# An expert-weight ring over all staging buffers, the spill branch between the expert groups, and a one-hot scatter in two passes

## The chip, the cores and the metric

The kernel runs on one core of one Trainium2 chip. The metric is the time of one execution on the device in microseconds, taken as the median of several runs. All data is 32-bit; TensorE (PE) multiplies it either as plain float32 or, where both operands are typed fp32r, in one shortened pass. Where full precision is wanted from fp32r, the kernel splits a value into a high part and a low remainder and multiplies both.

## The reference, cut to what matters

Two decoder layers over 256 tokens of width 1024. The change lies in the second layer's channel mixer, a top-2-of-8 mixture of experts, and in what follows it:

```python
def moe(x, router, wg, wu, wd):
    xt = x.reshape(-1, dm)
    logits = (xt @ router).astype(jnp.float32)
    top_v, top_i = lax.top_k(logits, TOP_K)
    w = jax.nn.softmax(top_v, axis=-1)
    gate = jnp.sum(jax.nn.one_hot(top_i, N_EXPERTS) * w[..., None], axis=1)
    for e in range(N_EXPERTS):
        out = out + gate[:, e:e + 1] * swiglu(xt, wg[e], wu[e], wd[e])
...
    h = h + f
    h = h + (p[i] @ ple_proj[i]) * jax.nn.sigmoid(rmsnorm(h, g_ple[i]) @ ple_gate[i])
return rmsnorm(h, g_final)
```

Each expert has three matrices of 1024 x 3584 in float32. All eight experts are read once: 336 pieces of 1 MiB.

## The kernel before

**Expert layer.** The experts are handled in two groups g of four. For each group a one-hot matrix `sm` (built on VectorE, DVE, by `select`) picks the tokens of its experts into 3 blocks of 128 slots: two blocks hold 64 fixed slots per expert, the third two units of 32 slots that go to whichever experts have more tokens. `gather` multiplies the token matrix (as the pair `xhi`, `xlo`) by the one-hot into `xg`. Then seven column blocks m of 512 hidden columns follow: 8 stretches of `wg`, 8 of `wu`, and 8 of `wd` (two halves n of 4). A stretch is 1 MiB: 128 rows, 512 columns for each of the four experts. `quad` multiplies it: 8 matmuls with 512 columns, four of them side by side in the array, and 4 with 256 columns for the third block, whose weights `unit_weights` copies out of the stretch (one copy on ScalarE, ACT, one on DVE, with the expert's number read from a register). `turn` transposes the hidden block, `down` adds to the group's result `Y`. The down product of block m-1 stands behind the up product of block m. After a group's last `down`, `scatter` multiplies `Y` by the transposed one-hot `sT` (already scaled by the routing gate in `back`) in plain float32, and `settle` adds the result to the residual `h`.

**Weight buffers.** SyncE (SP) issues all weight loads, in order. `stretch` takes one of the 8 `raw` buffers of a pool (`load`, L167), used in turn; a load waits until the buffer's last reader is through. The first layers' weights use the same pool, and also split each raw buffer into `hi` and `lo` (3 buffers each; `split`, L193 and L194). In the expert layer `hi` and `lo` serve only for the small unit copies (L1028, L1029). Once, after the eighth stretch, three spare tiles (`pp`, `Y`, `xn`; L1017) are filled as well.

**Spill.** Tokens that do not fit into the blocks would be handled by `spill`, inside `tc.If` on a flag that is read from the routing. It stands twice, one behind the other, between the last block's `turn` and its `down`. In the runs here the flag is zero and both are skipped. Instructions behind a `tc.If` are not moved ahead of it; otherwise the framework's scheduler orders the instructions of each engine.

**After the experts.** `aside` is the embedding projection (`ple_proj`: one 1 MiB weight load, split, 24 matmuls), placed in the last column block. Then `ple` follows in a written order: it loads four 1 MiB pieces of the gate matrix (`gate_of`), splits the first two, settles the second half of the last scatter, transposes and multiplies, adds to `h`, and the final norm goes out. `Norm.gains` (L242) loads a norm's gain vector, and L780 the input `p`.

Of the kernel before, what the change touches and what calls it, by code (L numbers as in the profile page):

```python
# [92 lines left out]
def trunk(ctx: ExitStack, tc: tile.TileContext, a, cst, at, out, stop=None):  # L93
# [66 lines left out]
    def load(src, shape, behind=None, parts=1):  # L160

        n = shape[0] * shape[1]
        raw = rawp.tile([128, 2048], F32, name="raw")
        v = raw[:, :n].rearrange("p (a b) -> p a b", b=shape[1])
        m = shape[0] // parts
        for j in range(0, shape[0], m):
            order(nc.sync.dma_start(v[:, j:j + m], src[:, j:j + m]), behind)  # L167
        return raw, v
# [60 lines left out]
    class Norm:  # L229
# [10 lines left out]
        def gains(self, c=slice(0, D)):  # L240
            n = c.stop - c.start
            nc.sync.dma_start(self.g[:, c], bass.AP(tensor=self.src.tensor, offset=self.src.offset + c.start,  # L242
                                                    ap=[[0, 128], [1, n]]))
            return self
# [532 lines left out]
    def ple_proj(i, pool, keep, name="pT", bufs=1, out="pp"):  # L777

        pin = nrm.tile([128, NT, PLE], F32, name="junk")
        nc.sync.dma_start(pin, a["p"][i, 0].rearrange("(t p) d -> p t d", p=128))  # L780
# [52 lines left out]
    def moe(i, pool, N, after, aside):  # L833
# [106 lines left out]
        def select(g):  # L940
# [15 lines left out]
            return [g, sm, None, None, xp.tile([128, KC, 3, 128], F32, name="xg")]  # L956

        def factors(G):

            g, sm = G[:2]  # L960
            G[2] = gs = xp.tile([128, 4, 2], F32, name="gs", bufs=2)
# [9 lines left out]
            own = xp.tile([128, 4, GRP], F32, name="own", bufs=2)  # L971
            mask = xp.tile([128, 2, GRP], F32, name="mask", bufs=2)
            nc.vector.tensor_copy(gs[:, 0:3, 0], pv[:, :, GRP])
            nc.vector.tensor_copy(gs[:, 3, 0:1], gs[:, 2, 0:1])
# [5 lines left out]
            for half in range(2):  # L980
                nc.vector.scalar_tensor_tensor(own[:, 2 + half], pv[:, 2, 0:GRP], K["half"][:, half:half + 1], mask[:, 0],
                                               op0=ALU.mult, op1=ALU.mult)
# [3 lines left out]
        def back(G):  # L986

            sm, gs = G[1:3]
            G[3] = sT = xp.tile([128, 4, S], F32, name="sT")
            for b in range(3):  # L990
# [3 lines left out]
                for j in ((b,) if b < 2 else (2, 3)):  # L994
                    nc.scalar.activation(sT[:, j], p[:, 0:S], AF.Copy, scale=gs[:, j, 1:2])
# [12 lines left out]
        count, held = [0], {}  # L1008
# [15 lines left out]
        def unit_weights(g, w):  # L1024

            hi = hip.tile([128, 2048], F32R, name="hi").bitcast(F32)[:, 0:512]
            lo = lop.tile([128, 2048], F32R, name="lo").bitcast(F32)[:, 0:512]
            nc.scalar.copy(hi, w[:, bass.ds(units[g][0], 1), :].rearrange("p e n -> p (e n)"))  # L1028
            nc.vector.tensor_copy(lo, w[:, bass.ds(units[g][1], 1), :].rearrange("p e n -> p (e n)"))  # L1029
            return hi, lo  # L1030
# [11 lines left out]
        def column(src, G, m, new, ahead=None):  # L1042
# [3 lines left out]
            for k in range(KC):  # L1046
                w = stretch(src[G[0], m, k])
                if ahead is not None and k + 1 < KC:
# [4 lines left out]
        def turn(H):  # L1053
            hT = xp.tile([128, 4, 3, 128], F32, name="hT", bufs=2)
# [13 lines left out]
        def down(G, m, hT, Y, n, new):  # L1068

            P = [new() for b in range(3)]  # L1070
            for c in range(4):
                w = stretch(wd[G[0], m, n, c])
                quad(G[0], P, hT[:, c], w, c == 0, c == 3)
            for b in range(3):
                y = Y[:, b, n * WIDE[b]:(n + 1) * WIDE[b]]
# [5 lines left out]
        def scatter(G, Y, t, n, p):  # L1081

            for b in range(2):
                nc.tensor.matmul(p, G[3][:, b, t * 128:(t + 1) * 128], Y[:, b, n * 512:(n + 1) * 512], start=(b == 0),  # L1084
                                 stop=False, skip_group_check=True)
            for half in range(2):
                nc.tensor.matmul(p[:, half * 256:half * 256 + 256], G[3][:, 2 + half, t * 128:(t + 1) * 128],  # L1087
                                 Y[:, 2, n * 256:(n + 1) * 256], start=False, stop=True, skip_group_check=True)
# [6 lines left out]
        def spill(base):  # L1095
# [8 lines left out]
            sg = xp.tile([128, 512], F32, name="H0")  # L1104
# [5 lines left out]
            def fetch(src):  # L1110
# [4 lines left out]
            for e in range(NE):  # L1115
# [22 lines left out]
                for m in range(FCH):  # L1138
                    po = []
                    for src in (wg, wu):  # L1140
                        po.append(bank())
                        for k in range(KC):
                            fetch(src[g, m, k, :, j, :])
# [8 lines left out]
                    for c in range(4):  # L1152
                        for n in range(2):
                            fetch(wd[g, m, n, c, :, j, :])
# [19 lines left out]
        Y = xp.tile([128, 3, D], F32, name="Y")  # L1174
        pp = xp.tile([128, 2048], F32, name="pp")
        spare = [pp, Y.rearrange("p b n -> p (b n)")[:, 0:2048], nrm.tile([128, 2048], F32, name="xn")]
        ahead_of = {j: (wg, wu)[j // KC][0, 0, j % KC] for j in range(RAWS, 2 * KC)}
# [6 lines left out]
        for g in range(NE // GRP):  # L1184
            for m in range(FCH):
                first, final = g + m == 0, g + 1 == NE // GRP and m + 1 == FCH
                if m == 0 and g:
                    G = select(g)
# [10 lines left out]
                if last is not None:  # L1199
                    for t in range(NT):  # L1200
                        for n in range(2):
                            settle(t, n, scatter(last, Y, t, n, bank()))
# [154 lines left out]
```

## Time and profile before

| | us |
|---|---|
| median of 3 runs | 1515.51 |
| lowest, highest | 1510.32, 1520.99 |
| profiled execution | 1517.39 |
| its span | 1515.6 |

Over the span PE is busy 1449.3 us (96%), DVE 642.1 (42%), ACT 569.8 (38%), and the DMA engines move 462.39 MB, on average 305 GB/s. PE's busy time overlaps from one matmul to the next and is no measure of how full the array is; the expert layer, from about 615 to 1476 us, is better read by what its stretches wait for and by the DMA rate in each stage. Times in rows are microseconds from the span's start.

### The profile page before, as it was taken

Reading aid. Unit: us, or ns where it says so; the run is one execution under the profiler, and the core shown is the slowest. Engines: PE = TensorE matmul, PEld = TensorE weight load, DVE = VectorE, ACT = ScalarE, POOL = GpSimd, SP = SyncE. Lnnn points to the kernel's source line nnn. Section 1 sums busy time; section 2 is a strip of 40 time slices with the busy share of each in tenths; the row PEclk is TensorE's granted clock in tenths of the full one; section 3 lists DMA queues with packets and bytes.
Section 4 is the critical chain, followed back from the end, with each engine's and each line's share of the span. In section 5 each row is a group of like instructions: output and inputs, shape, how many; then the busy total and the mean of one; then the engine's idle time right before and its main releaser. Section 6 shows DMA issues by size and latency. Waiting matters only on the chain. (4 is left out here: it accounts for less than half of the span.)

```text
span 1515.6 us, 30676 instructions
## 1 busy us (share of the span) xinstructions
PE 1449.3 (96%) x12570; PEld 832.9 (55%) x12570; DVE 642.1 (42%) x1459; ACT 569.8 (38%) x992; POOL 2.3 (0%) x8
## 2 busy tenths in 40 slices
PE   7999999999999999899999999999999999999987
PEld 6977899999889868433322232243333323323336
DVE  6765865555596767323222222222221322322337
ACT  5452544434464543333332332333233223223324
POOL 0000000000000000000000000000000000000000
PEclk9998999999999999899999999999999999999999
DMA  9923445555557513789999999999999999999971
GB/s 332 365 86 97 160 167 194 190 179 188 169 179 252 199 57 146 250 346 420 420 420 420 419 421 420 420 419 416 405 383 420 420 419 420 419 421 420 412 273 42
DMA packets 100621, 462.39 MB, mean 305 GB/s; under 512 B 9384, under 2 KB 20336, under 8 KB 57200
## 3 DMA queue, kind: packets, MB, share of 16 engines
q1 hardware_dynamic: 100224, 460.16, 77.5%
q8 instruction: 102, 1.67, 0.4%
q14 instruction: 55, 0.45, 0.1%
q10 hardware_dynamic: 240, 0.10, 0.0%
HBM read 459.19 MB, written 1.05 MB: 304 GB/s over the span
## 5 line engine op out<-in xcount | busy, mean ns | idle before, releaser
L1029 DVE COPY lo<-raw 128x512 f32 x333 | 140.7, 426 | 544.5 <-DMA raw<-in_moe_up 152.3
L1028 ACT COPY hi<-raw 128x512 f32 x333 | 204.0, 621 | 429.5 <-DMA raw<-in_moe_down 129.2
L194 DVE TENSOR_TENSOR lo<-raw,hi 128x1024 fp32r<-128x1024 f32 (+1 forms) x176 | 206.6, 1200 | 111.7 <-ACT hi L193 111.1
L193 ACT CAST hi<-raw 128x1024 fp32r<-128x1024 f32 (+1 forms) x176 | 175.0, 1031 | 170.0 <-issue 71.8
L1039 PE MATMUL w<-raw,xg 128*32 128x512 f32 x1744 | 211.5, 596 | 12.3 <-DMA raw<-in_moe_up 5.0
L1039 PE MATMUL acc<-raw,xg 128*32 128x512 f32 x1792 | 214.7, 596 | 2.5 <-DMA raw<-in_moe_gate 0.6
L207 PE MATMUL w<-xhi,hi 128*128 128x256 f32 x704 | 201.2, 286 | 0.3 <-ACT xhi L283 0.3
L209 PE MATMUL w<-xhi,lo 128*128 128x256 f32 x704 | 199.9, 284 | 0.0
L208 PE MATMUL w<-xlo,hi 128*128 128x256 f32 x704 | 199.7, 284 | 0.2 <-DVE xlo L284 0.2
L207 PEld LDWEIGHTS w<-xhi,hi 128*128 128x128 f32 x704 | 135.0, 192 | 2.4 <-issue 1.6
L208 PEld LDWEIGHTS w<-xlo,hi 128*128 128x128 f32 x704 | 135.0, 192 | 1.3 <-issue 0.8
L209 PEld LDWEIGHTS w<-xhi,lo 128*128 128x128 f32 x704 | 135.0, 192 | 0.8 <-issue 0.8
L1039 PE MATMUL acc<-raw,hT 128*32 128x512 f32 x960 | 116.6, 603 | 11.6 <-PEq L1225 6.6
L1039 PEld LDWEIGHTS w<-raw,xg 128*32 128x32 f32 x1744 | 51.8, 109 | 117.1 <-issue 66.2
L1039 PEld LDWEIGHTS acc<-raw,xg 128*32 128x32 f32 x1792 | 50.8, 109 | 98.7 <-issue 74.8
L1039 PE MATMUL w<-raw,hT 128*32 128x512 f32 x832 | 99.7, 597 | 4.8 <-DMA raw<-in_moe_down 1.4
L1039 PE MATMUL w<-hi,xg 128*32 128x256 f32 x448 | 72.8, 379 | 0.0
L1039 PE MATMUL w<-lo,xg 128*32 128x256 f32 x448 | 68.1, 379 | 0.0
L1039 PE MATMUL acc<-hi,xg 128*32 128x256 f32 x448 | 68.1, 379 | 0.0
L1039 PE MATMUL acc<-lo,xg 128*32 128x256 f32 x448 | 68.1, 379 | 0.0
L1039 PEld LDWEIGHTS acc<-raw,hT 128*32 128x32 f32 x960 | 28.4, 110 | 67.9 <-issue 38.0
L1039 PEld LDWEIGHTS acc<-hi,xg 128*32 128x32 f32 x448 | 27.6, 110 | 67.1 <-issue 55.9
(346 smaller groups left out, 1908.2 us busy)
## 6 DMA issues: line engine op xcount, KB each, us to landing
raw<-in_moe_gate SPq DMA_DIRECT2D x112, 1024.0 KB, 17.7
raw<-in_moe_down SPq DMA_DIRECT2D x112, 1024.0 KB, 17.8
raw<-in_moe_up SPq DMA_DIRECT2D x109, 1024.0 KB, 17.0
raw<-in_w_in SPq DMA_DIRECT2D x23, 1024.0 KB, 6.8
raw<-in_ffn_gate SPq DMA_DIRECT2D x14, 1024.0 KB, 5.1
raw<-in_ffn_up SPq DMA_DIRECT2D x14, 1024.0 KB, 5.1
raw<-in_ffn_down SPq DMA_DIRECT2D x14, 1024.0 KB, 5.0
raw<-in_cmp_w SPq DMA_DIRECT2D x8, 1024.0 KB, 8.8
```

The lines of the kernel that those rows point to most:

```text
L193: order(nc.scalar.copy(hi[:, c], raw), b[0])
L194: order(nc.vector.tensor_tensor(lo[:, c], raw, hi[:, c].bitcast(F32), op=ALU.subtract), b[1])
L207: order(nc.tensor.matmul(o, l[0], r[0], start=start, stop=False, skip_group_check=skip), behind)
L208: nc.tensor.matmul(o, l[0], r[1], start=False, stop=False, skip_group_check=skip)
L209: nc.tensor.matmul(o, l[1], r[0], start=False, stop=stop, skip_group_check=skip)
L1028: nc.scalar.copy(hi, w[:, bass.ds(units[g][0], 1), :].rearrange("p e n -> p (e n)"))
L1029: nc.vector.tensor_copy(lo, w[:, bass.ds(units[g][1], 1), :].rearrange("p e n -> p (e n)"))
L1039: nc.tensor.matmul(P[b][o:o + UNIT, 0:WIDE[b]], x[:, b, o:o + UNIT], v, start=start, stop=stop, tile_position=(0, o), skip_group_check=True)
```

## The change

- **Ring.** The raw buffers, the three `hi` and the three `lo` form one ring of 14 buffers for expert stretches (`fetch`). The spares are now two: `pp` and the new `Y` (5 x 512 columns instead of 3 x 1024). `unit_weights` gets tiles of its own, two of each; `hT` has one buffer instead of two.
- **Order of two other loads.** The gain vectors and `p` are ordered behind the first load of the first group's second column block (`marks["late"]`).
- **Spill.** One `tc.If` between the groups, holding both spills. Ahead of it 13 stretches of the second group are fetched; `select` and the eight gathers of that group stand behind it.
- **Projection.** `aside` runs in the second group's column block 2.
- **Scatter.** `sT` is the plain one-hot in fp32r; the routing gate is multiplied in when H is formed. In each group's last block `down` splits `Y` into a high and a low part, and `scatter` makes a pass for each. At the end both halves of `down` come first, then the scatter of half 0, then that of half 1.

```diff
+        RING = RAWS + 2 * PARTS
         def stretch(src):
-            raw = held.pop(count[0], None)
-            if raw is None:
-                raw, _ = load(src, (GRP, 512))
-            if count[0] == RAWS - 1:
-                for j, x in enumerate(spare):
-                    nc.sync.dma_start(x, ahead_of[RAWS + j].rearrange("p e n -> p (e n)"))
-                    held[RAWS + j] = x
+            return held.pop(0) if held else fetch(src)
+        def fetch(src):
+            j = count[0]
             count[0] += 1
+            if RAWS <= j < RAWS + len(spare):
+                raw = spare[j - RAWS]
+                nc.sync.dma_start(raw, src.rearrange("p e n -> p (e n)"))
+            else:
+                n = j % RING if j < RAWS else (j - RAWS - len(spare) + RAWS) % RING
+                if n < RAWS:
+                    raw, _ = load(src, (GRP, 512))
+                else:
+                    pool_, name = ((hip, "hi"), (lop, "lo"))[(n - RAWS) // PARTS]
+                    raw = pool_.tile([128, 2048], F32R, name=name).bitcast(F32)
+                    marks["load"] = nc.sync.dma_start(raw, src.rearrange("p e n -> p (e n)"))
...
-            hi = hip.tile([128, 2048], F32R, name="hi").bitcast(F32)[:, 0:512]
-            lo = lop.tile([128, 2048], F32R, name="lo").bitcast(F32)[:, 0:512]
+            two = [xp.tile([128, 512], F32, name=f"wu{u}", bufs=2) for u in range(MORE)]
...
+            if m == FCH - 1:
+                hi = nrm.tile([128, 2048], F32R, name=("xhi", "xlo")[n])
...
+                if hi is not None:
+                    z = hi[:, 512 * b:512 * b + WIDE[b]]
+                    nc.scalar.copy(z, y)
+                    lo.append(G[6][:, 2 * n + b] if b < 2 else hi[:, 1280:1536])
+                    nc.vector.tensor_tensor(lo[b], y, z.bitcast(F32), op=ALU.subtract)
...
-                nc.tensor.matmul(p, G[3][:, b, t * 128:(t + 1) * 128], Y[:, b, n * 512:(n + 1) * 512], start=(b == 0),
-                                 stop=False, skip_group_check=True)
+                nc.tensor.matmul(p, G[3][:, b, q], hi[:, 512 * b:512 * b + 512], start=(b == 0), stop=False,
+                                 skip_group_check=True)
+                nc.tensor.matmul(p, G[3][:, b, q], lo[b], start=False, stop=False, skip_group_check=True)
...
-        spare = [pp, Y.rearrange("p b n -> p (b n)")[:, 0:2048], nrm.tile([128, 2048], F32, name="xn")]
+        spare = [xp.tile([128, 2048], F32, name="pp"), Ys[:, 0:2048]]
...
                 if m == 0 and g:
+                    flag = nc.values_load(ovi[0:1, 0:1], min_val=0, max_val=S)
+                    for j in range(RING - 1):
+                        held.append(fetch((wg, wu)[j // KC][g, 0, j % KC]))
+                    with tc.If(flag > 0):
+                        spill(0)
+                        spill(128)
                     G = select(g)
                     for k in range(KC):
                         gather(G, k)
...
-                    nc.vector.tensor_tensor(v, v, ou[b][:, 0:WIDE[b]], op=ALU.mult)
+                    nc.vector.scalar_tensor_tensor(v, ou[b][:, 0:WIDE[b]], G[2][:, b, 1:2], v, op0=ALU.mult, op1=ALU.mult)
...
+                if g and m == 2:
+                    aside(xp)
                 if final:
                     N2 = after()
-                    aside(xp)
-        flag = nc.values_load(ovi[0:1, 0:1], min_val=0, max_val=S)
         hT = turn(H)
-        with tc.If(flag > 0):
-            spill(0)
-        with tc.If(flag > 128):
-            spill(128)
         down(G, m, hT, Y, 0, acc)
-        for t in range(NT):
-            settle(t, 0, scatter(G, Y, t, 0, bank()))
+        down(G, m, hT, Y, 1, acc)
+        for t in range(NT):
+            settle(t, 0, scatter(G, t, 0, bank()))
             N2.part(t, HALF[0])
-        down(G, m, hT, Y, 1, acc)
```

## Rows read from the trace of the kernel before

**Rows 1.** The page's slices (40 equal parts of the span): DMA rate

```profile
GB/s 332 365 86 97 160 167 194 190 179 188 169 179 252 199 57 146 250 346 420 420 420 420 419 421 420 420 419 416 405 383 420 420 419 420 419 421 420 412 273 42
```

**Rows 2.** Windows: stretch, length, busy us (count) by engine, PE clock, DMA share, GB/s

```profile
590.00:660.00 70.00, 61.36 (x556) 33.08 (x559) 29.73 (x137) 25.94 (x49) 0.00 (x0) 0.90 0.67 245
660.00:1000.00 340.00, 326.62 (x3394) 106.50 (x3390) 84.61 (x196) 107.02 (x189) 0.00 (x0) 1.00 1.01 420
...
1085.00:1125.00 40.00, 39.43 (x370) 14.38 (x362) 8.41 (x19) 13.35 (x26) 0.00 (x0) 1.00 0.97 369
1125.00:1435.00 310.00, 298.85 (x3112) 96.88 (x3108) 77.39 (x170) 97.18 (x171) 0.00 (x0) 1.00 1.01 420
1435.00:1455.00 20.00, 11.96 (x72) 6.20 (x68) 5.27 (x8) 5.41 (x8) 0.00 (x0) 0.83 0.63 236
```

**Rows 3.** Timeline of DVE, 650 to 700: start, length, instruction, [idle before it, releaser]

```profile
672.76 0.43 DVE L1029 COPY lo<-raw 128x512 f32 x1 [1.72 <-PE acc L1039]
674.91 0.43 DVE L1029 COPY lo<-raw 128x512 f32 x1 [1.72 <-PE acc L1039]
679.54 0.43 DVE L1029 COPY lo<-raw 128x512 f32 x1 [4.21 <-PE w L1039]
```

**Rows 4.** Timeline of SP's queue, 520 to 660

```profile
589.72 0.38 SPq L1017 DMA_DIRECT2D Y<-in_moe_up  x1
597.75 0.33 SPq L242 DMA_DIRECT2D gb<-in_g_ple  x1
...
613.05 0.33 SPq L1017 DMA_DIRECT2D xn<-in_moe_up  x1
616.72 13.05 SPq L167 DMA_DIRECT2D raw<-in_moe_up  x5
```

**Rows 5.** Timeline of PE, 580 to 660

```profile
595.87 0.28 PE L209 MATMUL w<-hi,xs 128*128 128x256 f32 x1
...
614.54 2.06 PE L1039 MATMUL acc<-raw,xg 128*32 128x512 f32 x16
...
617.86 1.92 PE L1039 MATMUL acc<-raw,xg 128*32 128x512 f32 x16
```

**Rows 6.** The first branch's line, L1223: instruction, count, ns min/median/max, first and last start

```profile
L1223 SPq EVENT_SEMAPHORE  x8: 17/17/17, 1434.1 to 1444.3; - x8
...
L1223 PEldq COMPARE_BRANCH  x1: 4676/4676/4676, 1440.9 to 1440.9; - x1
```

**Rows 7.** DVE's groups by line and shape, 1472 to 1486: busy us, mean ns

```profile
L194 DVE TENSOR_TENSOR lo<-raw,hi 128x1024 fp32r<-128x1024 f32 x4 | 4.7, 1220 | 2.8 <-ACT hi L193 2.8
L1077 DVE TENSOR_TENSOR Y<-acc,Y 128x512 f32<-128x512 f32 x2 | 1.4, 693 | 0.8 <-PE acc L1039 0.8
L258 DVE TENSOR_TENSOR xn<-h,gb 128x512 f32<-128x512 f32 x2 | 1.4, 692 | 0.1
```

**Rows 8.** Timeline of DVE, 1428 to 1458

```profile
1449.38 0.43 DVE L1029 COPY lo<-raw 128x512 f32 x1 [7.27 <-DVEq L1225]
```

**Rows 9.** Timeline of DVE, 694 to 701: first and last of the selection's instructions

```profile
695.47 0.74 DVE L946 TENSOR_SCALAR sm<-pack,pos 128x64 fp32r<-128x64 f32 x4
...
698.68 0.73 DVE L954 SCALAR_TENSOR_TENSOR sm<-pack,dpos,sm 128x128 fp32r<-128x128 f32 x2
```

**Rows 10.** The second branch's line, L1225

```profile
L1225 SPq EVENT_SEMAPHORE  x8: 17/17/17, 1447.0 to 1447.5; - x8
```

**Rows 11.** Timeline of ACT, 1455 to 1516

```profile
1462.61 0.62 ACT L1028 COPY hi<-raw 128x512 f32 x1 [1.69 <-DMA raw<-in_moe_down]
```

**Rows 12.** Timeline of PE, 1428 to 1458

```profile
1450.65 3.64 PE L1039 MATMUL acc<-raw,hT 128*32 128x512 f32 x16 [6.63 <-PEq L1225]
```

**Rows 13.** Timeline of PE, 1455 to 1516

```profile
1476.22 1.98 PE L1084 MATMUL w<-Y,sT 128*128 128x512 f32 x4
...
1482.76 0.50 PE L207 MATMUL acc<-hi,xhi 128*128 128x512 f32 x1 [0.24 <-ACT xhi L283]
```

**Rows 14.** Chain that ended last, 1430 to 1516: start, length, what

```profile
1484.22 0.23 PE acc L208
```

More of the change, by code (lines that the diff above doesn't have):

```diff
@@ L166, in load @@
         for j in range(0, shape[0], m):
-            order(nc.sync.dma_start(v[:, j:j + m], src[:, j:j + m]), behind)
+            marks["load"] = order(nc.sync.dma_start(v[:, j:j + m], src[:, j:j + m]), behind)
         return raw, v
@@ L241, in gains @@
             n = c.stop - c.start
-            nc.sync.dma_start(self.g[:, c], bass.AP(tensor=self.src.tensor, offset=self.src.offset + c.start,
-                                                    ap=[[0, 128], [1, n]]))
+            order(nc.sync.dma_start(self.g[:, c], bass.AP(tensor=self.src.tensor, offset=self.src.offset + c.start,
+                                                          ap=[[0, 128], [1, n]])), marks.get("late"))
             return self
@@ L779, in ple_proj @@
         pin = nrm.tile([128, NT, PLE], F32, name="junk")
-        nc.sync.dma_start(pin, a["p"][i, 0].rearrange("(t p) d -> p t d", p=128))
+        order(nc.sync.dma_start(pin, a["p"][i, 0].rearrange("(t p) d -> p t d", p=128)), marks.get("late"))
         pb = bank()
@@ L979, in factors @@
                                     op=ALU.mult)
-            for half in range(2):
-                nc.vector.scalar_tensor_tensor(own[:, 2 + half], pv[:, 2, 0:GRP], K["half"][:, half:half + 1], mask[:, 0],
-                                               op0=ALU.mult, op1=ALU.mult)
+            nc.vector.tensor_tensor(own[:, 2], pv[:, 2, 0:GRP], mask[:, 0], op=ALU.mult)
             nc.vector.tensor_reduce(gs[:, :, 1], own, axis=AX.X, op=ALU.add)
@@ L993, in back @@
                     nc.tensor.transpose(p[:, t * 128:(t + 1) * 128], sm[:, t, b].bitcast(F32), ident)
-                for j in ((b,) if b < 2 else (2, 3)):
-                    nc.scalar.activation(sT[:, j], p[:, 0:S], AF.Copy, scale=gs[:, j, 1:2])
+                if b < 2:
+                    nc.scalar.copy(sT[:, b], p[:, 0:S])
+                    continue
+                for half in range(2):
+                    nc.scalar.activation(sT[:, 2 + half], p[:, 0:S], AF.Copy, scale=K["half"][:, half:half + 1])
         def gather(G, k):
@@ L1047, in column @@
                 w = stretch(src[G[0], m, k])
+                if G[0] == 0 and m == 1 and "late" not in marks:
+                    marks["late"] = marks["load"]
                 if ahead is not None and k + 1 < KC:
@@ L1173, in moe @@
                   marks["selm"] if t else None)
-        Y = xp.tile([128, 3, D], F32, name="Y")
-        pp = xp.tile([128, 2048], F32, name="pp")
-        spare = [pp, Y.rearrange("p b n -> p (b n)")[:, 0:2048], nrm.tile([128, 2048], F32, name="xn")]
-        ahead_of = {j: (wg, wu)[j // KC][0, 0, j % KC] for j in range(RAWS, 2 * KC)}
+        Ys = xp.tile([128, 5 * 512], F32, name="Y")
+        Y = [Ys[:, 0:D], Ys[:, D:2 * D], Ys[:, 2 * D:]]
+        spare = [xp.tile([128, 2048], F32, name="pp"), Ys[:, 0:2048]]
         units = []
@@ L1201, in moe @@
                         for n in range(2):
-                            settle(t, n, scatter(last, Y, t, n, bank()))
+                            settle(t, n, scatter(last, t, n, bank()))
                     last = None
```

49 lines of the change are left out of this document (28 added, 21 removed).

## Prediction

> **What bounds the kernel now.** I read the page's slices first, to see which resource is flat at its ceiling and where it is not. From slice 19 to slice 37 the rate stands at about 420 GB/s, but for a dip in slices 28 to 30 [rows 1]: this is the expert layer, whose 336 weight stretches of 1 MiB stream through eight raw buffers. A stretch at 420 GB/s is 1.048/0.420 = 2.5 us. Then I read the windows by stage [rows 2]: 420 GB/s in 660-1000 and in 1125-1435, where PE still has idle time (326.6 us busy of 340), but 245 GB/s in 590-660, 369 in 1085-1125 and 236 in 1435-1455. So the expert layer is bound by DMA, and what DMA did not move in the three holes is lost: 70 x (1-245/420) = 29.2 us, 40 x (1-369/420) = 4.9 us, 20 x (1-236/420) = 8.8 us. Third I checked how far PE is from being the bound. When weights are there, PE takes one stretch each 2.15 us, and the transposes between two columns cost 679.54-674.91-2.15 = 2.5 us [rows 3]. One of the 14 column blocks is 24 stretches: PE 24 x 2.15 + 2.5 = 54.1 us, DMA 59.9 us. PE has 5.8 us of slack in each block, no more.
>
> **First hole, the start.** Before PE takes its first stretch at 614.54, SP has issued the eight raw buffers, pp and Y by 589.7; then it issues the norm gains at 597.75 and behind them the p input, and the third spare, xn, only at 613.05. The next load waits for PE to release a raw buffer, at 616.72 [rows 4, 5]. So 11 stretches are out by then, and DMA runs dry before it. Afterwards there are 14 ring buffers and two spares. The six new ones are hi and lo, last read by the w_out matmul that starts at 595.87 [rows 5], so SP can issue them at about 597. From 589 the eight loads pp, Y, 3 hi, 3 lo need 8 x 2.5 = 20 us and are in by about 611, ahead of 616.72. That is 16 stretches instead of 11: -5 x 2.5 = -12.5 us. The gains (128 x 1024 x 4 B = 0.52 MB) and p (0.26 MB), which ran in the hole, go behind the "late" mark into the DMA-bound stretch: +0.78/0.42 = +1.9 us. Sum -10.6. If pp and the new Y overlay a mixer tile that is let go only at 596, the eight loads end at 617 and the term keeps its size. Bounds: -12.5, and +2.5 if the six are not filled ahead, because xn is no longer a spare. Once the ring is full PE is the slower side until its slack has eaten the stock; this costs nothing, because DMA always has released buffers to fill.
>
> **Second hole, the group boundary and the branch.** The spill branch moves from the end to the boundary. What a branch does shows at the end of the old trace: PE's COMPARE_BRANCH takes 4.68 us [rows 6], and SP runs eight semaphore instructions between 1434.1 and 1444.3 [rows 6] while DMA runs dry. I read them as one for each of SP's DMA semaphores, each waiting until the load before it has landed: nothing is issued until all is in. Afterwards SP issues 13 of the next group's loads ahead of the branch. They cover 13 x 2.5 = 32 us. The work that they must cover: DVE's last three adds, 0.69 or less each [rows 7], and its branch, half of the 7.27 us that two held it [rows 8], together about 5.5 us; the selection, which used to run early beside other work and now stands behind the branch, 695.47 to 699.4, 4 us for 16 instructions [rows 9]; eight gathers, bounded by the first column's 617.86-614.54-2.15 = 1.2 us each [rows 5], 9.4 us. Sum about 19 us, with PE's own 4.7 us inside it. 32 is more than 19, so PE has eaten some five stretches when SP comes back, and SP can issue at once. What is left is the drain itself. At the end two branches cost 8.8 us; the second held SP from 1444.3 to 1447.5 [rows 6, 10] with nothing left to drain, 3.2 us. One branch: 5.6 us, bounds 3.2 and 8.8. The old boundary's 4.9 us go, since 14 buffers bridge 35 us where eight bridged 20. Net +0.7.
>
> The Trainium skill, page "Runtime: NRT & Kernel Launch", section "Instruction fetch mechanics", says that a taken branch to a target outside the fetch window forces a DMA fetch of the target page before the engine goes on. The 4.68 us row agrees with a stall of that kind; by this rule alone a moved branch costs PE what it cost before and one of the two stalls goes, which lies under the 32 us here, so by it the sum stays the same.
>
> **Third hole, the end.** With the branch gone, the last eight loads follow without a gap: -8.8 us. The projection (1 MiB of weights) goes to block 2 of the second group. Its transfer moves from one DMA-bound place to another, 0. Its PE work, 24 matmuls at 0.23 = 5.5 us [rows 14] and about 2 for transposes, is covered there by slack. PE's debts in the second group are 19-5.6 (boundary), 7.5 (projection), 4 x 1.4 (scatter, below), and 3 allowed for factors and `back`: 29.5 us against 7 x 5.8 = 41 us. If that cover were gone PE would be late by the difference, and the last column with it. The projection also takes one raw, one hi and one lo out of turn, which shortens the ring to 13 for one round; a ring of eight kept 420 GB/s, so 0.
>
> **The tail.** An ACT copy waits at 1462.61 for the last but one stretch [rows 11], so the last lands at about 1465, and the span ends 50.5 us later. PE is not waiting for it: it is late from the projection, from the branches (6.63 us idle [rows 12]) and from a scatter between the two downs; its last expert matmul ends at 1476.2 [rows 13]. Afterwards PE is DMA-bound there and ends 2.5 us after the landing. From that end to the first matmul of the gate projection took 1482.76-1476.22 = 6.5 us [rows 13]. Now the bound is DVE, in order: adds and subtractions for hi and lo of the last half, of which about 2.5 us lie behind PE's end; settling half 0, four passes at 0.69 = 2.8; four splits of the gate weights at 1.22 = 4.9 [rows 7], which used to be partly done by then; settling the first tile of half 1, 1.4; transposes 0.5. Sum 12.1. PE's scatter is under it: eight one-pass matmuls instead of four plus, at 0.23 us for 512 columns [rows 14], 4 x 0.23 + 4 x 0.115 = 1.4 us for each of four, against 5.3 us for two before. Behind the first gate matmul 32.8 us stay as they are. New tail 2.5+12.1+32.8 = 47.4; term -3.1. Bounds: -8.6 if the splits find room ahead (PE then sets 6.6), +3 if they wait for their weights, which now land only 2.5 to 5 us behind the last stretch.
>
> At no cost: two buffers instead of three for the unit copies (0.62 us on ACT [rows 11], started two stretches ahead, so some 3.4 us before use); one hT buffer (the earlier down has ended); the multiplication by the gate in H (same DVE instruction count, 0.69 either way); six more ACT and DVE passes for the first group's hi and lo (in slack).
>
> **The sum.** -10.6 + 0.7 - 8.8 - 3.1 = -21.8 us. The profiled execution has a span of 1515.6 and a time of 1517.39; the median of the three runs, 1515.51 (1510.32 to 1520.99), lies 1.9 below that time. Taken from the median: 1493.7, so 1494 us.
>
> **Rivals.**
> 1. The target page's fetch goes over the same DMA engines as 13 queued MiB and comes only when they have drained. Both old branches were timed with a queue that ran dry, so no row excludes it. PE and DVE then start at 30 us, the first release comes at 30+4+9.4+2.2 = 45 us, and DMA stands for another 11 us: 1505. Against it: the engines fetch code all through the 420 GB/s stretch, and no row shows a stall from it. 0.13. The Trainium skill, page "Runtime: NRT & Kernel Launch", section "Instruction fetch mechanics", is where the page fetch by DMA is described; how it fares behind a full queue it does not say.
> 2. The new buffers are not filled ahead, by a release that comes later than 597 or by another order on SP: -10.6 becomes +2.5: 1507. 0.09.
> 3. The gate weights and the DVE queue make the tail some 6 us longer, the upper bound of that term: 1500. 0.10.
> 4. Slower: the unit copies with two buffers hold PE. PE's own end is 614.5 + 9.4 + 14 x 2.5 + about 37 for boundary, scatter and projection + 336 x pitch = 696 + 336 x pitch. At 2.15 that is 1418, below the DMA-bound end of 1465 - 10.6 + 0.7 - 8.8 + 2.5 = 1449. It begins to bite at a pitch of 2.24, eats the whole gain at 2.30, and at 2.35 gives 1486 + 12.1 + 32.8 = 1531. For it: only 0.09 us of pitch are spare. Against it: 0.62 us of copying with 3.4 us of lead. 0.08.
>
> **How the numbers follow.** Forecast 0.60, its own range 1486 to 1499. Measurements of this kernel tell about 1% from no change, that is 1500 or less. Faster: the forecast, most of rival 3 and a little of the others, 0.70; within 1%: 0.22; slower: 0.08. The range runs from the forecast with most of the shorter tail taken (1494 - 5.5 is 1488) and the branch at its lower bound (-2.4), less 1 us of the runs' spread, 1485, to rival 2, 1507.
>
> **What would show it.** Right: 16 stretches issued before PE's first release, one DMA hole of 5 to 6 us at the boundary with PE restarting before SP does, 420 GB/s from there to the last weight, PE ending some 2.5 us behind it, and about 12 us to the first gate matmul. Wrong: a hole of more than 9 us at the boundary, PE busy without DMA waits in the last blocks (rival 4), or hi and lo loads issued after 617.

## The result, and the profile after

The changed kernel takes 1500.24 us (median; 1494.27 to 1501.42) against 1515.51, a ratio of 0.9893 with a 95% interval of 0.9856 to 0.993. Measured again beside the last version below, it came to 0.9898 (0.9876 to 0.9921). The forecast was 1494: right in sign, 6 us too fast, inside the whole range (1485 to 1507) and just outside the forecast's own (1486 to 1499).

The profiled execution has a span of 1492.5 us and a time of 1494.27. In the fourteen profiles of this case the first expert matmul starts either at 606.3 to 608.5 us or at 614.2 to 615.4 us; the changed kernel, profiled twice, shows both (607.69 and 614.20), so this is not the change's doing. Times are therefore counted here from the first expert matmul, 614.54 before [rows 5] and 607.69 after. From there to the end it is 901.1 us before and 884.8 after: 16.3 us won in these two executions, close to the 15.3 of the medians.

The slices of the changed kernel first (DMA rate, 40 equal parts of the span), to be held against [rows 1], then its windows (stretch, length, busy us by engine, PE clock, DMA share, GB/s), to be held against [rows 2]:

```profile
GB/s 335 372 88 99 174 187 193 177 196 181 174 177 250 198 58 216 278 366 419 420 419 420 419 420 419 420 346 420 419 420 420 358 422 418 421 420 419 420 368 43
```

```profile
585.00:660.00 75.00, 66.35 (x616) 34.17 (x618) 27.47 (x127) 25.44 (x46) 0.00 (x0) 0.89 0.80 301
660.00:985.00 325.00, 318.74 (x3382) 111.46 (x3370) 83.47 (x182) 107.28 (x189) 0.00 (x0) 1.00 1.01 420
985.00:1005.00 20.00, 13.29 (x92) 9.12 (x84) 6.86 (x27) 5.83 (x11) 0.00 (x0) 0.83 0.73 282
1005.00:1180.00 175.00, 173.42 (x1817) 68.09 (x1816) 46.90 (x105) 59.71 (x108) 0.00 (x0) 1.00 1.01 419
1180.00:1195.00 15.00, 13.32 (x104) 7.03 (x106) 5.17 (x10) 7.11 (x12) 0.00 (x0) 1.00 0.69 274
1195.00:1445.00 250.00, 239.39 (x2450) 76.56 (x2446) 66.83 (x143) 77.26 (x135) 0.00 (x0) 1.00 1.01 420
```

The expert layer still runs at 420 GB/s, and the last hole of before is gone. There are two inner holes now: one at the group boundary, 20 x (1-282/420) = 6.6 us, which was forecast at 5.6, and one at 1180 to 1195, 15 x (1-274/420) = 5.2 us, which was not forecast.

**The start.** SP's queue (start, length, instruction, count):

```profile
587.93 0.42 SPq L1022 DMA_DIRECT2D pp<-in_moe_up  x1
588.41 0.42 SPq L1022 DMA_DIRECT2D Y<-in_moe_up  x1
588.93 1.15 SPq L1030 DMA_DIRECT2D hi<-in_moe_up  x2
590.13 0.47 SPq L1030 DMA_DIRECT2D lo<-in_moe_up  x1
610.53 22.16 SPq L167 DMA_DIRECT2D raw<-in_moe_gate  x8
633.61 0.33 SPq L242 DMA_DIRECT2D gb<-in_g_ple  x1
```

All 16 stretches are out by 590.6, before PE's first release at 610.5. The gains (`gb`) went at 633.61, into what is left of the start's hole (the rate is back at 420 GB/s from about 653), so of the 1.9 us set down for them and `p` only the share of `p` was paid, which went later: an estimate of 0.26/0.42 = 0.6 us.

**The boundary.** The branch's line (engine, instruction, count: ns min/median/max, first and last start):

```profile
L1218 SPq EVENT_SEMAPHORE  x8: 17/17/17, 990.4 to 993.3; - x8
...
L1218 SPq COMPARE_BRANCH  x1: 53/53/53, 973.5 to 973.5; - x1
L1218 ACTq COMPARE_BRANCH  x1: 54/54/54, 988.4 to 988.4; - x1
L1218 PEldq COMPARE_BRANCH  x1: 3764/3764/3764, 989.3 to 989.3; - x1
```

SP is at the branch at 973.5, with only two of the next group's loads issued ahead of it (970.60 and 973.09), not 13, though the fetches are written ahead of it: the scheduler let the branch go first. Then SP issues nothing until its eight semaphore instructions are through at 993.3. That is when its last two loads have landed: they take 19.8 us from issue, so they are in at 990.4 and 992.9, and the rate falls to nearly nothing.

```profile
raw<-in_moe_gate SPq DMA_DIRECT2D x2, 1024.0 KB, 19.8
990.00:992.00 2.00, 0.31 (x8) 0.00 (x0) 0.96 (x2) 0.62 (x1) 0.00 (x0) 1.00 0.34 131
992.00:994.00 2.00, 0.00 (x0) 0.00 (x0) 0.00 (x0) 0.62 (x1) 0.00 (x0) 1.00 0.05 16
```

(The first line is that of the two loads, with size and us to landing, the others are windows.) PE waits for the selection and starts again at 996.5, behind SP and not before it. Buffers were not what was missing: once through, SP issues eight loads by 999, and PE takes its next stretch only at 1005.6.

**The new hole.** SP's queue again, and what SP waited for from 1130 to 1215 (us in total, times, longest):

```profile
1156.46 0.38 SPq L780 DMA_DIRECT2D junk<-in_p  x1
1159.01 0.37 SPq L167 DMA_DIRECT2D raw<-in_ple_proj  x1
1161.50 7.61 SPq L167 DMA_DIRECT2D raw<-in_moe_gate  x2
1169.15 19.44 SPq L1030 DMA_DIRECT2D hi<-in_moe_gate  x3
1188.64 2.20 SPq L1030 DMA_DIRECT2D lo<-in_moe_gate  x3
```

```profile
SPq L1030 <- DVE lo L194: 14.3, 1, 14.3
...
SPq L1030 <- PE w L209: 3.8, 1, 3.8
```

The ring comes to the three `hi` buffers five loads after the projection's weights. The third `hi` is the one that the projection's split holds until its matmuls are through (PE L207 to L209, up to 1188.2). Most of SP's wait, 14.3 of 18.1 us, ends with the split itself (L194): the buffer was set aside for weights issued only at 1159.0, which landed at about 1177 and were split from 1181 on. SP issues in order, so the loads of all other buffers stand behind it.

**The end.** ACT, PE and DVE (start, length, instruction, idle before it and its releaser):

```profile
1443.95 0.62 ACT L1038 COPY wu<-lo 128x512 f32 x1 [1.88 <-DMA lo<-in_moe_down]
```

```profile
1444.05 1.92 PE L1049 MATMUL acc<-hi,hT 128*32 128x512 f32 x16
1446.56 0.28 PE L1116 MATMUL w<-xhi,sT 128*128 128x256 f32 x1
1446.79 0.28 PE L1116 MATMUL w<-xhi,sT 128*128 128x256 f32 x1
1447.00 1.92 PE L1049 MATMUL acc<-lo,hT 128*32 128x512 f32 x16
...
1457.98 0.63 PE L280 MATMUL w<-pack,xn 128*128 128x128 f32 x4 [3.66 <-DVE xn L258]
1458.37 0.47 PE L207 MATMUL acc<-hi,xhi 128*128 128x512 f32 x1
```

```profile
1448.65 1.61 DVE L1094 TENSOR_TENSOR Y<-acc,Y 128x512 f32<-128x512 f32 x3
1450.17 1.28 DVE L1101 TENSOR_TENSOR xg<-Y,xlo 128x512 fp32r<-128x512 f32 x2
1451.38 0.42 DVE L1101 TENSOR_TENSOR xlo<-Y,xlo 128x256 fp32r<-128x256 f32 x1
1451.87 4.63 DVE L194 TENSOR_TENSOR lo<-raw,hi 128x1024 fp32r<-128x1024 f32 x4
1456.42 0.68 DVE L1121 TENSOR_TENSOR h<-w,h 128x512 f32<-128x512 f32 x1
```

PE's last expert matmul ends at 1449.1, 5.2 us behind the landing: the scatter of half 0 stands between the last stretches (L1116). From there to the first gate matmul at 1458.37 it is 9.25 us, and DVE fills them as forecast: adds, subtractions, four splits, the settling; the settling of half 0 was already over.

### The profile page after: what moved, and what is told of

Same layout as the page of the kernel before. It is cut to its first block, busy times and chain, and to the rows that moved or that the text cites. A ratio compares the mean times of both kernels' runs of the same rounds, so it can differ in the third digit from the quotient of the medians.

```text
span 1492.5 us, 30637 instructions
## 1 busy us (share of the span) xinstructions
PE 1429.8 (96%) x12570; PEld 838.2 (56%) x12570; DVE 650.0 (44%) x1467; ACT 577.7 (39%) x1004; POOL 2.3 (0%) x8
## 5 line engine op out<-in xcount | busy, mean ns | idle before, releaser
L194 DVE TENSOR_TENSOR lo<-raw,hi 128x1024 fp32r<-128x1024 f32 (+1 forms) x176 | 206.5, 1200 | 108.5 <-ACT hi L193 107.8
L1038 ACT COPY wu<-raw 128x512 f32 x192 | 118.2, 620 | 260.5 <-PE acc L1049 68.2
L1039 DVE COPY wu<-raw 128x512 f32 x192 | 81.0, 426 | 308.6 <-PE acc L1049 104.5
L207 PE MATMUL w<-xhi,hi 128*128 128x256 f32 x704 | 201.2, 286 | 0.3 <-ACT xhi L283 0.3
L209 PE MATMUL w<-xhi,lo 128*128 128x256 f32 x704 | 199.9, 284 | 0.0
L207 PEld LDWEIGHTS w<-xhi,hi 128*128 128x128 f32 x704 | 135.0, 192 | 2.4 <-issue 1.6
L209 PEld LDWEIGHTS w<-xhi,lo 128*128 128x128 f32 x704 | 135.0, 192 | 0.8 <-issue 0.8
L1049 PE MATMUL acc<-raw,xg 128*32 128x512 f32 x1088 | 131.7, 599 | 1.1
L1049 PE MATMUL w<-raw,xg 128*32 128x512 f32 x928 | 115.6, 594 | 2.6
L1049 PE MATMUL w<-wu,xg 128*32 128x256 f32 x896 | 83.0, 379 | 0.0
L1038 ACT COPY wu<-hi 128x512 f32 x72 | 44.5, 619 | 93.4 <-PE w L1049 23.8
L1038 ACT COPY wu<-lo 128x512 f32 x70 | 43.4, 620 | 93.1 <-PE w L1049 23.6
L1049 PE MATMUL acc<-raw,hT 128*32 128x512 f32 x544 | 67.2, 595 | 2.5 <-DMA raw<-in_moe_down 0.8
L1049 PE MATMUL acc<-wu,xg 128*32 128x256 f32 x896 | 69.4, 379 | 0.0
L1049 PEld LDWEIGHTS w<-wu,xg 128*32 128x32 f32 x896 | 34.1, 110 | 62.0 <-issue 54.9
## 6 DMA issues: line engine op xcount, KB each, us to landing
raw<-in_moe_gate SPq DMA_DIRECT2D x68, 1024.0 KB, 19.8
raw<-in_moe_down SPq DMA_DIRECT2D x66, 1024.0 KB, 19.8
hi<-in_moe_up SPq DMA_DIRECT2D x27, 1024.0 KB, 19.8
lo<-in_moe_up SPq DMA_DIRECT2D x25, 1024.0 KB, 19.8
hi<-in_moe_down SPq DMA_DIRECT2D x24, 1024.0 KB, 19.8
```

Source lines behind the costliest of these rows:

```text
L194: order(nc.vector.tensor_tensor(lo[:, c], raw, hi[:, c].bitcast(F32), op=ALU.subtract), b[1])
L207: order(nc.tensor.matmul(o, l[0], r[0], start=start, stop=False, skip_group_check=skip), behind)
L209: nc.tensor.matmul(o, l[1], r[0], start=False, stop=stop, skip_group_check=skip)
L1038: nc.scalar.copy(two[0], w[:, bass.ds(units[g][0], 1), :].rearrange("p e n -> p (e n)"))
L1039: nc.vector.tensor_copy(two[1], w[:, bass.ds(units[g][1], 1), :].rearrange("p e n -> p (e n)"))
L1049: nc.tensor.matmul(P[b][o:o + UNIT, 0:WIDE[b]], x[:, b, o:o + UNIT], v, start=start, stop=stop, tile_position=(0, o), skip_group_check=True)
```

## The experiments

The argument behind them starts from a balance. Time lost in a stretch is its length times (1 - rate/420), added up over windows from 35 us before the first expert matmul to the landing of the last stretch; the columns end 200, 420, 560 and 620 us after that matmul and at the landing. "Scatter of group 1" is the window from 420 to 560 us, in which the first group's results are scattered while the second group's first column blocks run. "Land" is that landing, "end" the end of the execution, both from the first expert matmul, in each kernel's profiled execution. The landing is the start of ACT's copy that waits for the last stretch. In both forms of the kernel before it is 2.5 us, one stretch, after the last copy that waits; with the projection at the end it is the last issue plus its 10.7 us to landing.

| kernel | start | branch | scatter of group 1 | projection | rest | lost | land | land - lost | end |
|---|---|---|---|---|---|---|---|---|---|
| before | 39.4 | 0.2 | 5.0 | 0.1 | 9.1 | 53.8 | 850.6 | 796.8 | 901.1 |
| after | 26.3 | 6.5 | 0.0 | 5.3 | 0.3 | 38.5 | 836.3 | 797.8 | 884.8 |
| projection's own tiles | 27.1 | 6.5 | 0.0 | 0.3 | 0.2 | 34.2 | 833.0 | 798.8 | 881.2 |
| no spill | 25.6 | 0.1 | 0.0 | 4.3 | 0.2 | 30.1 | 827.5 | 797.4 | 875.9 |
| spill's loads on ACT | 26.5 | 6.0 | 0.0 | 6.3 | 0.2 | 38.9 | 836.7 | 797.8 | 886.0 |
| flag late | 26.9 | 5.8 | 0.3 | 4.3 | 0.2 | 37.5 | 835.2 | 797.7 | 883.8 |
| ring of eight | 40.8 | 6.4 | 3.7 | 0.1 | 0.3 | 51.3 | 850.3 | 799.0 | 898.8 |
| before, no spill | 40.0 | 0.1 | 5.0 | 0.0 | 0.1 | 45.2 | 843.1 | 797.9 | 892.8 |
| gate split later | 26.3 | 6.7 | 0.0 | 4.9 | 0.2 | 37.9 | 835.8 | 797.9 | 881.6 |
| projection at the end | 27.3 | 6.8 | 0.0 | 0.0 | 1.9 | 36.0 | 833.2 | 797.2 | 886.4 |
| three edits | 26.2 | 5.6 | 0.3 | 0.1 | 0.3 | 32.5 | 831.5 | 799.0 | 877.9 |
| three edits, no spill | 25.0 | 0.1 | 0.3 | 0.0 | 1.0 | 26.5 | 825.6 | 799.1 | 871.2 |

The landing less the loss is 797 to 799 in all twelve. This is bookkeeping and no proof of a cause: every kernel moves the same loads in this span, so what is left over is the time of the same bytes at 420 GB/s. It shows that no hole is missing from the table, and what each is worth in landing time. That the end follows the landing is a finding: where the tail is that of the changed kernel, end less land is 48.2 to 49.3 us (after, projection's own tiles, no spill, spill's loads on ACT, flag late, ring of eight), while the landing itself ranges from 827.5 to 850.3. What makes each hole is for the edits to show.

The medians below are given as ratios to the kernel before on the same chip. Their intervals reach some 3 to 5 us to each side, and of the edits to the changed kernel only the ring of eight and the last one, without the spill, stand clear of both of its own intervals (0.9856 to 0.993, and 0.9876 to 0.9921 the second time). The sizes of the smaller steps rest on one profiled execution each; the two kernels that were profiled twice ended 0.9 and 1.9 us apart.

**The projection's buffers.** The split goes into two tiles that are free there.

```diff
-        w = weights(a["ple_proj"][i].rearrange("(k p) n -> p k n", p=128), (2, 1024))
+        into = [nrm.tile([128, 2048], F32R, name=z) for z in ("xhi", "xlo")] if i else None
+        w = weights(a["ple_proj"][i].rearrange("(k p) n -> p k n", p=128), (2, 1024), into=into)
```

> The changed kernel, but the projection's weights are split into two tiles that are free at that time (xhi and xlo), not into buffers of the ring. Theory: the transfer hole at 1180-1195 (15 us at 274 GB/s instead of 420, 5.2 us) is SP standing at the ring's third load into hi, whose buffer the projection has taken and gives back only after its matmuls; the hole goes, the span between PE's first expert matmul and its last falls by about 5 us, the median from 1500 to about 1495. Rival: the hole comes from the projection's own loads or its PE work, which stay: hole and time unchanged.

SP's queue in this run:

```profile
1166.40 0.37 SPq L167 DMA_DIRECT2D raw<-in_ple_proj  x1
1168.88 8.38 SPq L167 DMA_DIRECT2D raw<-in_moe_gate  x2
1177.31 1.79 SPq L1030 DMA_DIRECT2D hi<-in_moe_gate  x3
```

The three `hi` loads leave within 1.79 us instead of 19.44, and the window from 1180 to 1200 moves 420 GB/s. The end comes 3.6 us sooner in the profile; the median is 1497.11, 0.9899 (0.9871 to 0.9927) of the kernel before, and does not resolve it. The buffer is the cause of the hole. Less is won than the 5.0 us of the hole: this execution lost 0.8 more at its start, and the rest is within the spread of the balance.

**The branch taken away.** Flag and spill are left out.

```diff
-                    with tc.If(flag > 0):
-                        spill(0)
-                        spill(128)
```

> The changed kernel without the flag and the spill between the groups (tokens that overflow the blocks would be lost; none do with these inputs). It prices the branch in the middle with all that hangs on it. Both theories: the hole at 985-1005 (6.6 us) goes, and the selection runs early again beside other work: about 1500 - 6.6 = 1493, the projection's hole stays. If the branch costs more than its hole, by making PE late for the rest of the group, the fall is 10 us or more.

The boundary hole is gone (0.1), the projection's stays (4.3); the end comes 8.9 us sooner, the median is 1493.18, 0.9878 (0.985 to 0.9906). So the branch costs the 6.4 us of its hole; of the further 2.5, 1.0 is less lost at the projection and 0.7 at the start, and the rest is within the spread of the balance.

**What holds SP at the branch.** Two runs. In one the loads inside the spill are issued by ScalarE, so that no skipped load is SP's own:

```diff
-                nc.sync.dma_start(raw, src)
+                nc.scalar.dma_start(raw, src)
```

> The changed kernel, but the loads inside the skipped spill are issued from ScalarE's queue instead of SyncE's. Nothing that runs is moved. Theory: at the branch SyncE stands because, for the loads that it skips, it must bring each of its DMA semaphores forward, and waits for the load before on each to land; with no skipped loads of its own it goes straight on, the 6.6 us hole at the boundary goes although PE still stands some 15 us for branch, selection and gathers: about 1493.5. Rival: the hole is PE's standstill (no buffers come free) or the fetch of code: hole and time unchanged, 1500.

```profile
L1218 SPq EVENT_SEMAPHORE  x8: 17/17/17, 997.3 to 1000.2; - x8
...
L1218 SPq COMPARE_BRANCH  x1: 53/53/53, 980.3 to 980.3; - x1
```

SP still stands for 20 us, the hole is 6.0, the median 1500.3 (0.9916, 0.9881 to 0.995). It is not because of skipped loads of its own. Why SP waits for its loads to land there stays open. In the other run the flag is copied behind the last addition of the first group, so that all 13 loads stand ahead of the branch, as the prediction had it:

```diff
+                    ovl = pool.tile([128, 1], I32, name="ovl")
+                    order(nc.vector.tensor_copy(ovl, ovi), marks["down"])
-                    flag = nc.values_load(ovi[0:1, 0:1], min_val=0, max_val=S)
+                    flag = nc.values_load(ovl[0:1, 0:1], min_val=0, max_val=S)
```

> The changed kernel, but the flag is copied by VectorE only after the last add ahead of the branch, and SyncE reads the copy: so all 13 loads of the next group stand ahead of the branch on SyncE, where only two do in the changed kernel. Theory (the drain sets the hole, however many loads are ahead): the hole stays at 5 to 7 us but comes some 25 us later, and PE stands on its work and not for weights; time 1498 to 1501. Rival (the hole is there because only two loads are ahead): the hole falls below 2 us, 1494.

```profile
L1220 SPq EVENT_SEMAPHORE  x8: 17/17/17, 1009.4 to 1019.6; - x8
...
L1220 PEldq COMPARE_BRANCH  x1: 6004/6004/6004, 990.6 to 990.6; - x1
...
L1220 SPq COMPARE_BRANCH  x1: 50/50/50, 1000.3 to 1000.3; - x1
```

PE in this run, its first stretch behind the branch:

```profile
1009.05 1.92 PE L1049 MATMUL acc<-raw,xg 128*32 128x512 f32 x16
```

The hole is as deep, 5.8, and only comes later (1010 to 1025); the median is 1499.14 (0.9917, 0.9889 to 0.9945). It makes no difference whether two or 13 loads are ahead: while SP stands, what is in flight drains, and the time until new loads run at full rate is lost. This run also speaks against PE's standstill as the cause of the hole: PE works on its stretches from 1009 on, one each 2.15 us, while the rate is down, so the hole goes with SP's standstill (1000.3 to 1019.6).

**The ring.** Only the eight raw buffers serve as the ring.

```diff
-        RING = RAWS + 2 * PARTS
+        RING = RAWS
```

> The changed kernel with the old ring size: the expert stretches use the eight raw buffers alone, so 10 stretches instead of 16 stand ahead of the first release, and 7 instead of 13 are fetched ahead of the spill branch; all else is as changed. Theory (the ring's term is real and kept to the end): six stretches of 2.5 us fewer at the start, +15; the boundary hole grows from 6.6 by up to 5, since fewer stretches bridge it; the hole at the projection goes, -5, because hi and lo are no part of the ring. From the first expert matmul to the end about 884.8 + 13 = 898 us, median about 1512. Rival (PE sets the end and the ring only moves waiting from PE to DMA): within 3 us of the changed kernel, 885 us. A third way (the six buffers only help at the start, and the boundary needs no more than eight): 884.8 + 15 - 5 = 895.

```profile
589.91 0.42 SPq L1022 DMA_DIRECT2D pp<-in_moe_up  x1
590.42 0.38 SPq L1022 DMA_DIRECT2D Y<-in_moe_up  x1
617.53 6.67 SPq L167 DMA_DIRECT2D raw<-in_moe_up  x3
```

Between 590.4 and 617.5 nothing is issued. The start loses 14.5 more (six stretches are 15), the boundary no more than with 14 buffers (6.4), the scatter of group 1 loses 3.7 again, and the projection's hole is gone: 898.8 us where 898 was expected; the median is 1516.51, 0.9986 (0.9968 to 1.0005). Without the ring next to nothing is left of the gain: 2.3 us of the profile's 16.3. So 898 was met in part by luck: the share that I gave to the boundary is in truth in the scatter's place. There SP waits for PE to release buffers; my reading is that PE is late from the gathers and four scatters, and that eight buffers don't bridge it, though the scatter is the cheaper one. No run puts the old scatter back, so what the two passes alone are worth is not shown.

**The branches at the old place.** The kernel before without its two branches.

```diff
-        with tc.If(flag > 0):
-            spill(0)
-        with tc.If(flag > 128):
-            spill(128)
```

> The kernel before with both spill branches and the flag's load left out (tokens beyond the blocks would be lost; here there are none). It prices the two branches at the old place. Theory (the branches stop the weight queue and the end is set by the queue): the hole of 8.8 us goes, and with PE's 6.6 us of idle behind the second branch nothing replaces it: 901.1 - 8.8 = 892 us from the first expert matmul to the end, median about 1502 against 1511. Rival (at the old end PE is late from the projection and the scatters, not from the queue): the weights land 8.8 us sooner and PE ends only 3 to 5 us sooner, about 897 us.

892.8 us, and 1509.24 against 1517.28 for the kernel before on that chip, 0.9933 (0.9906 to 0.9959): 8.3 us in the profile for two branches at the end. The term of 8.8 is confirmed. Moving the spill took away these and brought back 6.4 in the middle.

**The tail.** The second gate piece is split behind the settling of the first tile.

```diff
-            ready = [gate_of(i, u) for u in range(2)]
+            ready = [gate_of(i, 0)]
...
+            ready.append(gate_of(i, 1))
             add(1)
```

> The changed kernel with one edit in the tail: the split of the second piece of the gate weights (two subtractions on DVE of 1.16 us and two copies on ACT) is written behind the settling of the first tile instead of ahead of it. Theory (DVE's order sets the way from the last expert matmul to the first gate matmul, 9.25 us): that way gets 2.3 us shorter, to about 7, and 2 us of it reach the end: 882.8 us from the first expert matmul. Rival (PE's scatter and transposes set it): 9.25 stays within 0.5, and the end with it. Second rival (the second piece is then late for the gate matmuls): the way shortens but the stretch behind it grows from 34.1 by as much.

DVE in this run:

```profile
1458.33 2.36 DVE L194 TENSOR_TENSOR lo<-raw,hi 128x1024 fp32r<-128x1024 f32 x2
1460.61 0.68 DVE L1122 TENSOR_TENSOR h<-w,h 128x512 f32<-128x512 f32 x1
...
1464.39 2.36 DVE L194 TENSOR_TENSOR lo<-raw,hi 128x1024 fp32r<-128x1024 f32 x2 [0.25 <-ACT hi L193]
```

The way to the first gate matmul shrinks from 9.25 to 6.98 us, the rest from 34.1 to 33.7; 881.6 in all, 3.2 us sooner, of which 0.5 is an earlier landing; the median is 1497.9 (0.9868, 0.9843 to 0.9894). DVE's order set that way.

**The projection at the end again.** All else as changed.

```diff
-                if g and m == 2:
-                    aside(xp)
                 if final:
                     N2 = after()
+                    aside(xp)
```

> The changed kernel with the embedding projection back in the last column block of the second group; all else as changed. It prices the projection's move alone. Theory (PE is what a step in the last block delays, because nothing follows that could make it up): the hole of 5 us in block 2 goes, but 24 projection matmuls and their transposes, about 7.5 us, now stand on PE between the last stretches, and the buffer that the projection holds is short there: the last expert matmul ends about 2.5 us later than in the changed kernel, 887 us from the first expert matmul to the end, median about 1503. Rival (the work at the end is hidden, PE waiting there for the last stretches): the hole goes and nothing replaces it, 880 us, 1495.

PE at the end of this run:

```profile
1424.52 1.92 PE L1049 MATMUL w<-raw,hT 128*32 128x512 f32 x16 [0.16 <-DMA raw<-in_moe_down]
1429.84 1.23 PE L207 MATMUL w<-hi,sth 128*128 128x512 f32 x4 [2.38 <-ACT hi L193]
...
1437.41 1.93 PE L1049 MATMUL acc<-raw,hT 128*32 128x512 f32 x16
1439.58 1.90 PE L1049 MATMUL acc<-raw,hT 128*32 128x512 f32 x16
```

PE leaves the stretches at about 1426.5 and comes back at 1437.4. Its last expert matmul ends 9.1 us behind the landing instead of 5.2, which eats most of the hole that is saved: 886.4 us against 884.8 and, in a second profile of the changed kernel, 883.9. The medians say the opposite, 1495.52 against 1500.57 in the same comparison, but four of these five executions lie at 1495.0 to 1495.7 and the profiled one at 1503.63, so the median may rest on the stage ahead. The size and even the sign of the move's own worth stay open.

**Three edits together.** The projection's own tiles, the later gate split, and `xn` as a 17th stretch, issued last at the start.

```diff
+            last = RING + len(spare) - 1
-            if RAWS <= j < RAWS + len(spare):
-                raw = spare[j - RAWS]
+            if RAWS <= j < RAWS + len(spare) - 1 or j == last:
+                raw = spare[-1 if j == last else j - RAWS]
...
-        spare = [xp.tile([128, 2048], F32, name="pp"), Ys[:, 0:2048]]
+        spare = [xp.tile([128, 2048], F32, name="pp"), Ys[:, 0:2048], nrm.tile([128, 2048], F32, name="xn")]
```

> Three edits together on the changed kernel, nothing left out: the projection's split goes into tiles of its own (worth 3.6 us alone), the tile xn becomes a 17th stretch fetched ahead at the start (one stretch, 2.5 us), and the second piece of the gate weights is split behind the settling of the first tile (2 us). If the three holes are independent and what is saved in the queue is kept to the end: 884.8 - 8.1 = 877 us from the first expert matmul, median about 1492 where the kernel before is 1511 (0.987). If xn is free only after PE's first release the second part gives nothing: 879 us, 1494. If the saving in the middle is eaten by PE's own pace: no better than the projection edit alone, 881 us, 1497.

> The changed kernel itself, beside the best version on one chip and against the same runs of the kernel before: 0.989 of it, 884.8 us from the first expert matmul to the end.

> The version with the three edits (the projection's split in tiles of its own, xn as a 17th stretch ahead, the second gate piece split behind the settling of the first tile) a second time, beside the changed kernel: 7 us below it if the first measurement holds, 878 us from the first expert matmul to the end.

1494.29 us, 0.9846 (0.9824 to 0.9868); in the direct comparison 1493.56, 0.9852 (0.9828 to 0.9876), beside 1500.57 of the changed kernel, which is 7.0 us more. From the first expert matmul it is 877.9 and 876.0. The 17th stretch gives under 1 us of the 2.5, perhaps nothing: the start loses 26.2 (25.4 the second time), against 27.1 with the projection's own tiles alone, but 26.3 in the changed kernel. SP issues it only at 612.99, 4.9 us ahead of PE's first release.

**And without the spill.**

> The three edits of the best version together with the spill and its flag left out (tokens beyond the blocks would be lost; here there are none). It tells whether the holes add. Theory (DMA time lost is kept to the end, hole by hole): the best version's 877.9 us from the first expert matmul to the end less the 8.9 that leaving out the spill was worth alone: 869 us, median about 1486 where the kernel before is 1517 (0.979). Rival (with both holes gone PE, at 2.15 us for each stretch and with the scatters and gathers of the second group behind it, becomes what sets the end): 872 us or more.

871.2 us, the median 1488.7, 0.982 (0.9793 to 0.9848): 4.8 to 6.7 us below the two profiles with the spill, not 8.9. The end lies between what the theory (869) and the rival (872 or more) gave. The landing moves by what is no longer lost (5.9 and 6.0); PE's last expert matmul follows it by 5.2 us as in the changed kernel, so PE has not become the bound. What the 8.9 had beyond the hole itself did not come again.

## Why the prediction was right, and where its sizes were off

- **Start, forecast -10.6, measured -13.1.** 16 stretches instead of 11, -12.5, held. The +1.9 for gains and `p` failed: the gains ran in the hole that was left. The start's loss in the other profiles with the long ring is 25.6 to 27.3 where nothing was changed there, so this term is known to about 1 us.
- **Boundary, forecast +0.7, measured +6.5 - 5.0 - 0.2 = +1.3.** The drain was read rightly from [rows 6] and [rows 10]: eight semaphore instructions, nothing issued meanwhile. Wrong was that 13 stretches ahead would cover 32 us and PE restart before SP does. Two stood ahead, PE restarted after SP, and the late flag shows that 13 would not have helped. The old 4.9 went mainly because of the longer ring, as argued (3.7 us of it came back with eight buffers), but its place is the scatter of group 1.
- **Projection, forecast 0, measured +5.2.** The failed step: "The projection also takes one raw, one hi and one lo out of turn, which shortens the ring to 13 for one round; a ring of eight kept 420 GB/s, so 0." The number of free buffers was counted, not their order. SP issues in order, the third `hi` was due five loads later, and SP stood 18.1 us for it.
- **End hole, forecast -8.8, measured -8.8.** [rows 2] against 420 GB/s until the landing.
- **Tail from the landing, forecast 47.4, measured 48.5 (50.5 before).** PE ended 5.2 us behind the landing, not 2.5, and the rows show the scatter of half 0 between the last stretches. DVE's part was 9.25 instead of 12.1: the settling of half 0, set down with 2.8, was over by then. Behind the first gate matmul it was 34.1 instead of 32.8.
- **Sum.** -13.1 + 1.3 + 5.2 - 8.8 - 2.0 = -17.4; the measured -16.3 lies 1.1 away, which is the balance's spread (796.8 against 797.8). Against the forecast of -21.8 the projection's 5.2 is nearly all of the miss, but only because the others (-2.5 at the start, +0.6, +1.1, and the 1.1 of the balance) happen to cancel; that is luck.
- **Rivals.** The time alone, 1500.24, fits the third rival (1500) better than the forecast; only the traces tell them apart. The branch's code fetch behind a full queue: PE's branch took 3.76 us, and 6.0 with 13 loads issued ahead, not 30; it fell. "Not filled ahead" fell by SP's rows at 588 to 590. Two unit buffers: PE still takes a stretch each 2.15 us, so this fell as well. The longer tail came in part, +1.1 of +6.
- **Signs.** Of those named for being right only the 16 stretches came as written: the hole at the boundary was 6.6 instead of 5 to 6 with PE behind SP, a second hole broke the 420 GB/s, and PE's 2.5 and 12 us were 5.2 and 9.25. None of those named for being wrong appeared.

The Trainium skill, page "Runtime: NRT & Kernel Launch", section "Instruction fetch mechanics", was cited for the branch: a target outside the window costs a fetch. The 3.76 and 6.0 us on PE agree with a stall of that kind, though no run shows that the time is a fetch. The larger price here is another one, SP's wait.

## What to carry over

Where one queue feeds everything in order, write down for each buffer that leaves a ring not only that it is one fewer, but after how many loads its turn comes and when its borrower lets go. The skipped branch cost a drain of the queue here at both places, with two or 13 loads ahead of it, and whichever engine's queue the skipped loads belonged to; whether a skipped block without loads would do the same was not tried. Balance the bandwidth that was lost against the landing, so that no hole is overlooked (here it closed within 2.5 us in twelve kernels), and then find each hole's cause by an edit that takes it away.

## What was unexpected of the hardware

- SP runs eight semaphore instructions at a skipped branch and stands until its loads have landed (973.5 to 993.3), also where the skipped loads belong to ScalarE's queue (980.3 to 1000.2).
- The branch instruction itself is 45 to 72 ns on SP, ACT and DVE, and on PE 3.69 to 4.68 us, but 6.0 with the late flag.
